# Copies in PSUM for the low parts of three more weights, and one sum of squares a tick sooner, in a hybrid decoder block on Trainium2

## The chip, the cores and the metric

The kernel runs on one core of a Trainium2 chip. The metric is the device time of one execution in microseconds (us), given as the median of several executions. A core has five engines that run side by side: TensorE (PE in the profile, with its weight loads as PEld) multiplies matrices, VectorE (DVE), ScalarE (ACT) and GpSimd (POOL) work element by element, and SyncE (SP) issues the transfers. SBUF is the working memory, and PSUM the small memory in eight banks into which TensorE writes its sums.

## The reference

One layer over 512 tokens of width 2048: an RMS norm and one input projection, three token mixers (dilated attention, a convolution module, windowed attention), an output projection and the residual, and then a second RMS norm and a SwiGLU feed-forward part of width 5632. The change lies where the second norm meets the feed-forward part:

```
x = x + mix @ w_out[l]
h2 = _rms_norm(x, norm2_g[l])
x = x + (jax.nn.silu(h2 @ w_gate[l]) * (h2 @ w_up[l])) @ w_down[l]
```

## The kernel before, in words

Activations lie transposed, 128 channels by 512 tokens to a tile. The program is written out in order by Python code, and every engine executes its own instructions in exactly that order. What one engine needs of another is waited for with semaphores.

**Split weights.** Every fp32 weight tile of 128x1024 is split before use into a high part (`wh`, the tile rounded to fp32r) and a low part (`wl`, what the rounding lost), and TensorE multiplies with both. `split_up_to` does this two weights ahead of TensorE's use (`SPLIT_AHEAD`), in one of two ways. In the first (lines 244 and 245) ScalarE casts the weight into `wh`, and VectorE subtracts: `wl` = weight - `wh`, both inputs in SBUF. In the second (lines 247 to 250) ScalarE casts the weight twice, once into a copy in PSUM (`near`, in the trace `wn`) and once into `wh` in SBUF, and VectorE subtracts the PSUM copy from the weight. `wh` and `wl` have three buffers each (`SPLIT_BUFS`). The copies live in the pool `high`, which has two buffers of 128x1024.

**The feed-forward part** multiplies with a seven-product scheme (Strassen's). Each of its blocks, `g1`, `u1`, `g2`, `u2` and so on, takes seven weights in the order `ORDER` = (5, 1, 7, 6, 2, 4, 3). Four of the seven are sums of quarter matrices: in order they are the first s, 11, 21, s again, 12, 22, s again, where s is one buffer into which GpSimd adds more quarters between uses (`add`, line 193; for the first block some are VectorE's). I call them weights 1 to 7 of a block. With each weight TensorE does eight matmuls of 512 columns with `wh` and eight of 256 columns with `wl`. Which of the two comes first alternates: for weights 1 to 7 of `g1`, high, high, high, low, high, low, high (weights 1 and 2 are done in two halves each).

**The seam.** `g1` is the first block. While TensorE begins it, the last tiles of `x2` (the residual stream) are still being turned into operands: `add_x2` and `operands` run from a list of steps that fall due at ticks (`Ticks.after(n, ...)` queues a step n ticks ahead, and steps of one tick run in the order in which they were queued). The squares of all `x2` tiles are added into `ssum2` (the trace shows it as `ssum`), the last of them by VectorE. After weight 3, `norm2a` has TensorE add `ssum2` over the channels into the PSUM tile `n2s` (line 307), VectorE scales it (`n2v`, line 378) and GpSimd takes the power -1/2 (`n2r`, line 379). After weight 4, `norm2b` has TensorE spread the result over 128 partitions into the same tile (line 313), and ScalarE copies it to `r2b` (lines 969 and 970). The tile `n2s` occupies one of the two buffers of `high` from `norm2a` to the copies of `norm2b`. A block's finished products are taken out of PSUM by VectorE in `done`, one weight later.

The list of weights begins with `units`, those of the two projections. So `len(units)` is the number of weight 1 of `g1`, and `len(units) + len(ORDER)` that of weight 1 of `u1`. `next_unit` first runs the sums due, then the splits, then the loads (`pump`).

Of the kernel before, what the change touches and what calls it, by code (L numbers as in the profile page):

```python
# [64 lines left out]
ORDER = (5, 1, 7, 6, 2, 4, 3)  # L65
# [57 lines left out]
def kernel(ctx: ExitStack, tc: tile.TileContext, xT, wi, wo, wgu, wd, cst_in, outT):  # L123
# [18 lines left out]
    ticks = Ticks()  # L142

    def slot(name, dt=F32, cols=T):
        return sp.tile([P, cols], dt, name=name, tag="s")
# [8 lines left out]
    units = [wi[0][:, :T], wi[0][:, T:]] + [wi[u] for u in range(1, 2 * N_IN)]  # L154
# [15 lines left out]
    def drop(key):  # L170
        for buf in [b for b, k in held.items() if k == key]:
            held.pop(buf)
        return raws.pop(key)
# [61 lines left out]
    def split_up_to(i):  # L235
        while at["split"] <= min(i, len(works) - 1):
            key, last, eng = works[at["split"]]
            t, n = drop(key) if last else raws[key]
            u = at["split"]
            hi = wp.tile([P, 1024], F32R, name=f"wh{u}", tag="hi", bufs=SPLIT_BUFS)  # L240
            lo = wp.tile([P, 1024], F32R, name=f"wl{u}", tag="lo", bufs=SPLIT_BUFS)
            if eng or u < len(units) + len(ORDER):
                eng = eng or nc.vector
                nc.scalar.copy(hi[:, :n], t[:, :n])  # L244
                eng.tensor_sub(lo[:, :n], t[:, :n], hi[:, :n].bitcast(F32))  # L245
            else:
                near = psum["high"].tile([P, 1024], F32R, name=f"wn{u}", tag="h")
                nc.scalar.copy(near[:, :n], t[:, :n])
                nc.scalar.copy(hi[:, :n], t[:, :n])
                nc.vector.tensor_sub(lo[:, :n], t[:, :n], near[:, :n].bitcast(F32))  # L250
            splits[u] = (hi, lo)
            at["split"] += 1
# [5 lines left out]
    def next_unit(ahead=SPLIT_AHEAD):  # L258
        sums_now()
        u = at["use"]  # L260
        at["use"] += 1
        split_up_to(u + ahead)
        pump(RAW_EARLY if u < 20 else RAW_BUFS)
        return splits.pop(u)
# [16 lines left out]
    for k in range(X_AHEAD):  # L281
        load_first(k)
        u = k if k < 2 else k // 2 + 1
# [100 lines left out]
    for k in range(2):  # L384
        h_hl[k] = scaled(xs[k], col(C_G1 + k), "h", k)
        split_up_to(k)
# [427 lines left out]
    ssum2 = slot("ssum2")  # L814
# [12 lines left out]
    def halves(t):  # L827
        return t[:, :TH], t[:, TH:]
# [22 lines left out]
    def scale_x2(n):  # L851
        t = x2.pop(n)
        h2[n], sq = slot(f"h2_{n}"), slot(f"sr{n}")
        nc.scalar.activation(h2[n], t, AF.Copy, scale=col(C_G2 + n))  # L854
        if n < KT - 1:
            nc.scalar.activation(sq if n else ssum2, t, AF.Square)
            ticks.after(1, add_x2, n, sq)
        else:
            nc.vector.tensor_add(ssum2, ssum2, h2.pop("square"))
            ticks.after(1, nc.scalar.activation, sq, t, AF.Square)  # L860
            add_x2(n, sq)

    def add_x2(n, sq):
        j = n % NJ
        eng = nc.gpsimd if n < KT - 2 else nc.vector
        if n < NJ:
            tops[j] = slot(f"ta{j}")
            (h11, h12), n1 = halves(h2[j]), tops[j][:, :TH]
            eng.tensor_sub(n1, h11, h12)  # L869
            ticks.after(1, operands, j, (1, h11), (5, n1))  # L870
        else:
            (h11, h12), (h21, h22) = halves(h2.pop(j)), halves(h2.pop(n))
            ta, tb = tops.pop(j), slot(f"tb{j}")
            n3, (n2, n4) = ta[:, TH:], halves(tb)
            eng.tensor_sub(n3, h12, h22)
            eng.tensor_sub(n2, n3, h11)
            eng.tensor_add(n4, n2, h21)
            if n < KT - 1:
                ticks.after(1, operands, j, (7, n3), (6, n2), (2, h21))
                ticks.after(2, operands, j, (4, n4), (3, h22))  # L880
            else:
                ticks.after(0, operands, j, (7, n3), (6, n2))
                ticks.after(2, eng.tensor_add, ssum2, ssum2, sq)
                ticks.after(2, operands, j, (2, h21), (4, n4), (3, h22))
        if n == NJ - 1:
            ticks.after(1, nc.vector.tensor_add, ssum2, ssum2, sq)
        elif n == KT - 2:
            h2["square"] = sq
        elif 0 < n < KT - 1:
            ticks.after(1, eng.tensor_add, ssum2, ssum2, sq)  # L890
# [425 lines left out]
```

## Time and profile before

| | |
|---|---|
| median of 3 executions | 1894.49 us (1893.85 to 1895.07) |
| the profiled execution | 1893.63 us, its span 1891.8 us |
| TensorE busy | 1883.8 us (100% of the span) |
| VectorE, ScalarE, GpSimd busy | 1450.7, 1317.2, 1174.1 us |
| `g1` begins on TensorE | 597.0 us after the span's start |
| DMA | 317.67 MB, mean 168 GB/s |

The median stands 0.86 us above the profiled execution, and the profiled execution 1.8 us above its span. A row of the timeline gives start, duration, engine, line, operation, out<-in; behind it, in brackets, how long the engine was idle before it and what ended that. Rows that follow each other at once are merged (x8), and the duration of a merged row of matmuls reaches to the modelled end of the last, which overlaps with the next row's start. For TensorE the distance from one row's start to the next is therefore the better measure of what a row takes.

### The profile page before, as it was taken

To read this page: it belongs to the slowest core of one execution; us is meant where nothing else is said; L and a number is where in the kernel's file an instruction comes from. 1 tells how busy PE (TensorE), PEld (TensorE's weight loads), DVE (VectorE), ACT (ScalarE), POOL (GpSimd) and SP (SyncE) were. 2 spreads that over 40 slices of the span, in tenths; PEclk is the share of its full clock that TensorE was granted. 3 is DMA by queue.
4 is the path that set the end of the run, shared out by engine and by line. 5 is a ranking of instruction groups with operands and counts; after the bars stand their busy time and mean duration, and the time that the engine had idled before them with its cause. 6 is when DMAs were issued, how large, how long until landed. Compare 5 with 4: busy or idle time off the path is not lost.

```text
span 1891.8 us, 29715 instructions
## 1 busy us (share of the span) xinstructions
PE 1883.8 (100%) x10342; PEld 1638.5 (87%) x10342; DVE 1450.7 (77%) x2419; ACT 1317.2 (70%) x1841; POOL 1174.1 (62%) x795
## 2 busy tenths in 40 slices
PE   9999999999999999999999999999999999999999
PEld 7888888888888888888888888888888888888888
DVE  7788888997579777777777777777777876767777
ACT  6355654453465788888888788888887866666776
POOL 5134423331055878787778788788787654656777
PEclk9999999999999999999999999999999999999999
DMA  7343333334342354443544445454547766767777
GB/s 269 87 124 98 84 99 102 102 95 145 113 144 88 114 172 146 160 164 131 180 136 165 158 151 167 134 180 138 167 151 275 269 227 233 273 231 270 275 260 242
DMA packets 134246, 317.67 MB, mean 168 GB/s; under 512 B 15312, under 2 KB 30800, under 8 KB 134096
## 3 DMA queue, kind: packets, MB, share of 16 engines
q1 hardware_dynamic: 133952, 315.68, 50.2%
q8 instruction: 81, 1.33, 0.3%
q14 instruction: 69, 0.57, 0.1%
q10 hardware_dynamic: 144, 0.10, 0.0%
HBM read 252.28 MB, written 55.84 MB: 163 GB/s over the span
## 4 chain that ended last, share of the span: by engine, by line
PE 98%; DVE 1%; issue 0%; ACT 0%; DVEq 0%
PE out L1006 67%; PE o L267 3%; PE o L268 3%; PE o L269 3%; PE cq L267 2%; PE cq L269 2%; PE cq L268 2%; PE aq L267 1%; PE aq L269 1%; PE ak L267 1%; PE ak L269 1%; PE in L267 1%; PE av L269 1%; PE av L268 1%; PE av L267 1%; PE aq L268 1%
## 5 line engine op out<-in xcount | busy, mean ns | idle before, releaser
L1006 PE MATMUL out<-h,wh 128*128 128x512 f32 x2464 | 588.4, 391 | 0.0
L1006 PEld LDWEIGHTS out<-h,wh 128*128 128x128 f32 x2464 | 452.7, 188 | 87.5
L1006 PEld LDWEIGHTS out<-h,wl 128*128 128x128 f32 x2464 | 316.1, 191 | 14.7 <-DVE wl L245 2.7
L1006 PE MATMUL out<-h,wl 128*128 128x256 f32 x2464 | 320.4, 283 | 2.1 <-DVE wl L245 2.1
L1006 PE MATMUL out<-a,wh 128*128 128x512 f32 x1232 | 295.9, 391 | 0.0
L1006 PEld LDWEIGHTS out<-a,wh 128*128 128x128 f32 x1232 | 225.8, 188 | 43.3
L244 ACT CAST wh<-w 128x1024 fp32r<-128x1024 f32 (+1 forms) x93 | 96.6, 1042 | 120.0 <-PE o L268 43.2
L1006 PEld LDWEIGHTS out<-a,wl 128*128 128x128 f32 x1232 | 159.4, 191 | 7.0
L1006 PE MATMUL out<-a,wl 128*128 128x256 f32 x1232 | 161.7, 283 | 0.0
L245 DVE TENSOR_TENSOR wl<-w,wh 128x1024 fp32r<-128x1024 f32 (+1 forms) x93 | 117.6, 1265 | 48.5 <-ACT wh L244 46.8
L450 DVE SCALAR_TENSOR_TENSOR y<-bu,cst,y 128x511 f32<-128x511 f32 (+14 forms) x120 | 90.1, 751 | 0.6
L1019 DVE TENSOR_TENSOR y<-y,out 128x256 f32<-128x256 f32 x93 | 39.1, 420 | 43.4 <-PE out L1006 36.9
L267 PE MATMUL cq<-hh,wh 128*128 128x512 f32 x128 | 51.2, 400 | 0.0
L267 PE MATMUL o<-mh_c,wh 128*128 128x512 f32 x128 | 50.8, 397 | 0.0
L269 PE MATMUL cq<-hh,wl 128*128 128x512 f32 x128 | 50.0, 391 | 0.0
L269 PE MATMUL o<-mh_c,wl 128*128 128x512 f32 x128 | 50.0, 390 | 0.0
L268 PE MATMUL cq<-hl,wh 128*128 128x512 f32 x128 | 49.9, 390 | 0.0
L268 PE MATMUL o<-ml_c,wh 128*128 128x512 f32 x128 | 49.9, 390 | 0.0
L1020 DVE TENSOR_TENSOR y<-y,out 128x256 f32<-128x256 f32 x101 | 42.5, 421 | 3.4
L371 POOL TENSOR_TENSOR ssum<-ssum,sq 128x512 f32<-128x512 f32 x15 | 27.3, 1818 | 18.7 <-ACT sq L370 18.1
L680 POOL TENSOR_SCALAR a3e<-a3e,a3d 128x128 f32<-128x128 f32 (+3 forms) x8 | 8.6, 1086 | 43.6 <-DVE a3d L678 39.0
L869 POOL TENSOR_TENSOR ta<-h 128x256 f32<-128x256 f32 x8 | 7.5, 933 | 43.6 <-ACT h L854 43.6
(3124 smaller groups left out, 4988.2 us busy)
## 6 DMA issues: line engine op xcount, KB each, us to landing
a<-od SPq DMA_DIRECT2D x168, 256.0 KB, 5.2
od<-a SPq DMA_DIRECT2D x147, 256.0 KB, 5.1
w<-in_wi SPq DMA_DIRECT2D x59, 512.0 KB, 3.7
w<-in_wo SPq DMA_DIRECT2D x32, 512.0 KB, 3.6
yd<-y SPq DMA_DIRECT2D x68, 128.0 KB, 2.7
y<-yd SPq DMA_DIRECT2D x34, 256.0 KB, 5.2
x<-in_xT SPq DMA_DIRECT2D x16, 256.0 KB, 7.5
xr<-in_xT SPq DMA_DIRECT2D x16, 256.0 KB, 3.9
```

Source lines behind the costliest of these rows:

```text
L244: nc.scalar.copy(hi[:, :n], t[:, :n])
L245: eng.tensor_sub(lo[:, :n], t[:, :n], hi[:, :n].bitcast(F32))
L267: nc.tensor.matmul(out, wh, xh, start=start, stop=False)
L268: nc.tensor.matmul(out, wh, xl, start=False, stop=False)
L269: nc.tensor.matmul(out, wl, xh, start=False, stop=stop)
L371: eng.tensor_add(acc, acc, sq)
L450: nc.vector.scalar_tensor_tensor(yconv[j][:, i:], hconv[j][:, :T - i], c, yconv[j][:, i:], op0=ALU.mult, op1=ALU.add)
L680: nc.gpsimd.tensor_scalar(e[:, o:o + n], e[:, o:o + n], rd[:, i:i + 1], None, op0=ALU.mult)
L869: eng.tensor_sub(n1, h11, h12)
L1006: nc.tensor.matmul(out, lhs[:, s], rhs, start=begin, stop=last and low == flip[0] and x is xs[-1], skip_group_check=True)
L1019: sign(out, out if first is None else first, main)
L1020: sign(out, out, rest)
```

## The change

Two edits. The first lowers the bound below which a weight of the feed-forward part is split in the first way: weights 5, 6 and 7 of `g1` are now split in the second way, with a copy in PSUM. Weights 1 to 4 of `g1` stay as they were, and from `u1` on nothing differs. The second has VectorE add the square of the last `x2` tile into `ssum2` one tick sooner.

```
@@ split_up_to, line 242
-            if eng or u < len(units) + len(ORDER):
+            if eng or u < len(units) + 4:
                 eng = eng or nc.vector
                 nc.scalar.copy(hi[:, :n], t[:, :n])
                 eng.tensor_sub(lo[:, :n], t[:, :n], hi[:, :n].bitcast(F32))
             else:
                 near = psum["high"].tile([P, 1024], F32R, name=f"wn{u}", tag="h")
...
@@ add_x2, line 883
                 ticks.after(0, operands, j, (7, n3), (6, n2))
-                ticks.after(2, eng.tensor_add, ssum2, ssum2, sq)
+                ticks.after(1, eng.tensor_add, ssum2, ssum2, sq)
                 ticks.after(2, operands, j, (2, h21), (4, n4), (3, h22))
```

On ScalarE, from the last operand cast (`h`) to the copies of the second norm, there stood before two casts, one each for weight 5 (`12`) and weight 6 (`22`) of `g1`; the rows end with weight 7 (`s`) and the first copy for `u1`:

```order
L833 CAST h_7_6019<-h_15_5916 128x256
L244 CAST wh_6065<-w('12', 'g1')_5658 128x1024
L244 CAST wh_6069<-w('22', 'g1')_5509 128x1024
L969 COPY r2b<-n2s 128x512
L970 COPY r2b<-n2s 128x256
L244 CAST wh_6101<-w('s', 'g1')_5709 128x1024
L248 CAST wn_6125<-w('s', 'u1')_6058 128x1024
```

The same place on ScalarE now, with the engines whose semaphores each instruction waits for (DVE_49 is VectorE's, PE_49 TensorE's, Pool_49 GpSimd's, DMAHW a transfer's):

```order
L833 CAST h_7_6019<-h_15_5916 128x256
L248 CAST wn_6067<-w('12', 'g1')_5658 128x1024 [waits DMAHW6_49]
L249 CAST wh_6065<-w('12', 'g1')_5658 128x1024 [waits PE_49]
L248 CAST wn_6073<-w('22', 'g1')_5509 128x1024 [waits DVE_49]
L249 CAST wh_6071<-w('22', 'g1')_5509 128x1024 [waits PE_49]
L969 COPY r2b<-n2s 128x512 [waits PE_49]
L970 COPY r2b<-n2s 128x256
L248 CAST wn_6107<-w('s', 'g1')_5709 128x1024 [waits DVE_49,Pool_49]
L249 CAST wh_6105<-w('s', 'g1')_5709 128x1024 [waits Activation_49]
L248 CAST wn_6131<-w('s', 'u1')_6058 128x1024 [waits Activation_49,Pool_49]
```

Three casts into PSUM (`wn`) are new. Since `n2s` holds one buffer of `high`, the copies of weights 5, 6 and 7 take turns in the other: the copy of weight 6 waits for VectorE (its subtraction for weight 5), and the copies into `r2b` stand behind it.

On VectorE, at the end of the operands, weight 4 of `g1` (`wl` of `s`) and the last addition into the sum of squares (`ssum`) change places:

```order
 L834 TENSOR_TENSOR h_7_5985<-ta_5851,h_7_5985 128x256
 L834 TENSOR_TENSOR h_7_5988<-tb_5920,h_7_5988 128x256
-L245 TENSOR_TENSOR wl_6001<-w('s', 'g1')_5709,wh_6000 128x1024
 L103 TENSOR_TENSOR ssum_4224<-ssum_4224,sr_5917 128x512
+L245 TENSOR_TENSOR wl_6002<-w('s', 'g1')_5709,wh_6001 128x1024
 L834 TENSOR_TENSOR h_7_6013<-h_15_5916,h_7_6013 128x256
 L834 TENSOR_TENSOR h_7_6016<-tb_5920,h_7_6016 128x256
```

The addition now stands ahead of the subtraction; nothing else moved there.

A little further on VectorE, the subtractions for weights 5, 6 and 7 read `wn` where they read `wh`, in the same places between the evacuations of `g1` (L1019, L1020):

```order
 L1019 TENSOR_TENSOR g1r<-g1r,out_5925 128x256
 L1020 TENSOR_TENSOR g1r<-g1r,out_5925 128x256
-L245 TENSOR_TENSOR wl_6066<-w('12', 'g1')_5658,wh_6065 128x1024
-L245 TENSOR_TENSOR wl_6070<-w('22', 'g1')_5509,wh_6069 128x1024
+L250 TENSOR_TENSOR wl_6066<-w('12', 'g1')_5658,wn_6067 128x1024
+L250 TENSOR_TENSOR wl_6072<-w('22', 'g1')_5509,wn_6073 128x1024
 L1019 TENSOR_TENSOR g1u<-g1u,out_5928 128x256
 L1020 TENSOR_TENSOR g1u<-g1u,out_5928 128x256
-L245 TENSOR_TENSOR wl_6102<-w('s', 'g1')_5709,wh_6101 128x1024
+L250 TENSOR_TENSOR wl_6106<-w('s', 'g1')_5709,wn_6107 128x1024
```

Only the second input and the line changed; TensorE, GpSimd and the transfers keep their order.

More of the change, by code (lines that the diff above doesn't have):

```diff
@@ L241, in split_up_to @@
             lo = wp.tile([P, 1024], F32R, name=f"wl{u}", tag="lo", bufs=SPLIT_BUFS)
-            if eng or u < len(units) + len(ORDER):
+            if eng or u < len(units) + 4:
                 eng = eng or nc.vector
@@ L882, in add_x2 @@
                 ticks.after(0, operands, j, (7, n3), (6, n2))
-                ticks.after(2, eng.tensor_add, ssum2, ssum2, sq)
+                ticks.after(1, eng.tensor_add, ssum2, ssum2, sq)
                 ticks.after(2, operands, j, (2, h21), (4, n4), (3, h22))
```

## The prediction

> **What bounds the kernel now.** I read the page first, for the engine that sets the end, then TensorE's waits, then the chain of waits, and then the timeline around the only place that these name. The page:
>
> ```profile
> span 1891.8 us, 29715 instructions
> PE 1883.8 (100%) x10342; PEld 1638.5 (87%) x10342; DVE 1450.7 (77%) x2419; ACT 1317.2 (70%) x1841; POOL 1174.1 (62%) x795
> PE 98%; DVE 1%; issue 0%; ACT 0%; DVEq 0%
> ```
>
> TensorE is busy all the time and makes up 98% of the chain that ended last. No edit here takes a matmul away, so the change can only give back time in which TensorE stands still. The view of waits, for TensorE alone, lists all such waits of the span (engine, line, what it waited for: total, times, longest):
>
> ```profile
> PE out L1006 <- DVE wl L245: 2.1, 1, 2.1
> PE idle L355 <- DVE warm L353: 1.8, 1, 1.8
> PE n2s L307 <- DVE ssum L103: 0.4, 1, 0.4
> ```
>
> The first and third lie at the edited lines; the second is the start of the program. The chain, in order of time, ends thus:
>
> ```profile
> 605.20 0.68 DVE ssum L103
> ...
> 608.99 6.44 DVE wl L245 x2
> 615.48 1272.62 PE out L1006 x7312
> ```
>
> After 615.48 us TensorE runs through 1272.62 us to the end without waiting. What it gains before that point it keeps, as long as the feeding engines come forward with it. The seam on TensorE, by the timeline:
>
> ```profile
> 604.43 1.11 PE L1006 MATMUL out<-h,wl 128*128 128x256 f32 x8
> 605.94 1.05 PE L307 MATMUL n2s<-ones,ssum 128*128 128x1 f32 x8 [0.40 <-DVE ssum L103]
> 606.86 1.21 PE L1006 MATMUL out<-h,wl 128*128 128x256 f32 x8
> ...
> 609.74 0.60 PE L313 MATMUL n2s<-ident,n2r 128*128 128x128 f32 x4
> 610.10 2.09 PE L1006 MATMUL out<-h,wh 128*128 128x512 f32 x8
> 612.17 1.21 PE L1006 MATMUL out<-h,wl 128*128 128x256 f32 x8
> 615.48 1.21 PE L1006 MATMUL out<-h,wl 128*128 128x256 f32 x8 [2.09 <-DVE wl L245]
> 616.53 3.82 PE L1006 MATMUL out<-h,wh 128*128 128x512 f32 x16
> 620.18 2.08 PE L1006 MATMUL out<-h,wl 128*128 128x256 f32 x16
> 622.09 3.82 PE L1006 MATMUL out<-h,wh 128*128 128x512 f32 x16
> ```
>
> From start to start, sixteen high matmuls take 620.18 - 616.53 = 3.65 us and sixteen low ones 622.09 - 620.18 = 1.91 us; eight take 1.825 and 0.955. By these, TensorE lost 605.94 - (604.43 + 0.955) = 0.55 us ahead of the sum of squares (0.40 by the profile's modelled end), 612.17 - (610.10 + 1.825) = 0.24 us ahead of weight 5's low matmuls, and 615.48 - (612.17 + 0.955) = 2.35 us ahead of weight 6's. The eight after that stall took 616.53 - 615.48 = 1.05 us, 0.10 more than eight in a row. All together this is 3.24 us, the most that the change can win.
>
> Why weight 6's low part came so late stands on VectorE (DVE) and GpSimd (POOL):
>
> ```profile
> 604.07 1.22 DVE L245 TENSOR_TENSOR wl<-w('s', 'g1')_5709,wh 128x1024 fp32r<-128x1024 f32 x1
> 605.20 0.68 DVE L103 TENSOR_TENSOR ssum<-ssum,sr 128x512 f32<-128x512 f32 x1
> 607.41 0.15 DVE L378 TENSOR_SCALAR n2v<-n2s 128x4 f32<-128x4 f32 x1
> 608.99 3.12 DVE L245 TENSOR_TENSOR wl<-w('12', 'g1')_5658,wh 128x1024 fp32r<-128x1024 f32 x1
> 612.04 3.38 DVE L245 TENSOR_TENSOR wl<-w('22', 'g1')_5509,wh 128x1024 fp32r<-128x1024 f32 x1
> ...
> 607.64 1.02 POOL L379 TENSOR_TENSOR n2r<-n2v,nhalf 128x4 f32<-128x4 f32 x1 [15.73 <-DVE n2v L378]
> 608.63 2.40 POOL L193 TENSOR_TENSOR w('s', 'g1')_5709<-w('s', 'g1')_5709,w('12', 'g1')_5658 128x1024 f32<-128x1024 f32 x1
> 610.98 3.36 POOL L193 TENSOR_TENSOR w('s', 'u1')_6058<-w('21', 'u1')_5971,w('22', 'u1')_5973 128x1024 f32<-128x1024 f32 x1
> 614.41 3.27 POOL L193 TENSOR_TENSOR w('21', 'u1')_5971<-w('21', 'u1')_5971,w('11', 'u1')_5975 128x1024 f32<-128x1024 f32 x1
> ```
>
> With GpSimd idle, the subtraction took 1.22 us (weight 4, at 604.07). Beside GpSimd's additions it took 3.12 and 3.38, and the rows interlock: weight 5's ends at 612.11, 1.08 us after the first addition (611.03), the second addition ends at 614.34, and weight 6's at 615.42, again 1.08 us later. The two take turns, 6.50 us for what alone would be 2.44.
>
> **The change part by part.** The copies in PSUM first. Their price stands further on, where weights already go that way and GpSimd is adding at the same time:
>
> ```profile
> 621.40 1.01 ACT L248 CAST wn<-w('11', 'u1')_5975 128x1024 fp32r<-128x1024 f32 x1
> 622.34 1.04 ACT L249 CAST wh<-w('11', 'u1')_5975 128x1024 fp32r<-128x1024 f32 x1
> 622.44 1.22 DVE L250 TENSOR_TENSOR wl<-w('11', 'u1')_5975,wn 128x1024 fp32r<-128x1024 f32 x1 [1.15 <-ACT wn L248]
> 622.82 2.42 POOL L193 TENSOR_TENSOR w('s', 'u1')_6058<-w('s', 'u1')_6058,w('11', 'u1')_5975 128x1024 f32<-128x1024 f32 x1
> ```
>
> Subtraction and addition overlap from 622.82 to 623.66 and neither is longer than alone (1.22 and 2.42). So the subtractions fall from 3.12 and 3.38 to 1.22. What the change adds is three casts of 1.01 us on ScalarE (ACT), and a new wait: the copy of weight 6 must wait until the subtraction of weight 5 has read its buffer, with the copies into `r2b` and weight 7's casts queued behind it. ScalarE there, before:
>
> ```profile
> 602.42 0.63 ACT L103 ACTIVATE sr<-xr 128x512 f32<-128x512 f32 x1
> ...
> 604.82 1.04 ACT L244 CAST wh<-w('12', 'g1')_5658 128x1024 fp32r<-128x1024 f32 x1
> 605.77 1.04 ACT L244 CAST wh<-w('22', 'g1')_5509 128x1024 fp32r<-128x1024 f32 x1
> 610.38 0.59 ACT L969 COPY r2b<-n2s 128x512 f32<-128x512 f32 x1 [3.57 <-PE n2s L313]
> 610.86 0.38 ACT L970 COPY r2b<-n2s 128x256 f32<-128x256 f32 x1
> 611.12 1.06 ACT L244 CAST wh<-w('s', 'g1')_5709 128x1024 fp32r<-128x1024 f32 x1
> 614.37 1.02 ACT L248 CAST wn<-w('s', 'u1')_6058 128x1024 fp32r<-128x1024 f32 x1 [2.19 <-POOL w('s', 'u1')_6058 L193]
> ```
>
> Worked through: weight 5's casts start at 604.82 as now and end by 606.8, inside ScalarE's 3.57 us of idle time. Its subtraction keeps its start, 608.99, since VectorE is busy up to there, and ends at 610.20. A hand-over between engines takes 0.03 us (cast end 622.41, subtraction 622.44). So weight 6's copy runs from 610.23 to 611.24, its subtraction from 611.27 to 612.49, and TensorE can start on it 0.05 us later (as it did after 615.42), at 612.54 instead of 615.48: **2.94 us sooner**.
>
> Does TensorE reach that point by then? This is the second edit. The addition into `ssum` moves ahead of weight 4's subtraction; it is one VectorE instruction without a transfer, and its input is there (`sr` ends at 603.05). It starts at 604.07 and ends at 604.75, before TensorE is free at 605.39, so TensorE's wait goes. Weight 4's subtraction then ends near 605.9; it is wanted after the eight `n2s` matmuls (606.86 - 605.94 = 0.92 us), at 605.39 + 0.92 = 606.31: 0.4 us of cover. `n2v` and `n2r` gain nothing, since VectorE's own queue brings `n2v` to 607.41. TensorE goes on, by the distances of the rows, to 609.19 for the spread (`n2r` ends at 608.66), 609.55 for weight 5's high matmuls, 611.38 for its low ones (there since 610.20), and is at weight 6 by 612.33; with the profile's 0.40 in place of 0.55, by 612.48. It then waits 0.06 to 0.21 us for 612.54. With the addition left in its place it would come at 612.88, and the gain would be 2.60. So the sum is 2.60 for the copies and 0.34 for the tick; the tick alone, with the late subtraction still in place, would be worth nothing.
>
> What is late next: weight 6's second cast ends near 612.2, the two `r2b` copies take until 612.9, weight 7's two casts until 614.9. Weight 7's high part is wanted at 612.54 + 0.955 + 1.825 = 615.32, 0.4 us later. `r2b` is first read by GpSimd after its three additions; these, no longer held up, are through near 608.63 + 3 x 2.42 = 615.9. GpSimd's sum for weight 1 of `u1` is ready at 613.5 instead of 614.34, so that its copy on ScalarE is ready near 615.8 and its subtraction by 617.0, against a need at 615.32 + 1.825 + 0.955 = 618.1. From there all engines are about 2.9 us earlier than before, and their distances to each other stay.
>
> One rule speaks against the copies. The Trainium skill's page Perfetto Trace Analysis, section Optimizing Scalar/DVE Operations, puts the overhead of a VectorE instruction at about 60 ns for SBUF and about 125 ns for PSUM, and that of ScalarE at about 93 and 51 ns. By it the two subtractions would cost 0.13 us more and the copy between them 0.04 less, and the gain would be 2.85 us, an estimate from that page. The rows here show no difference: 1.22 us from SBUF alone (604.07) and 1.22 us from PSUM (622.44), and the sum goes by the rows.
>
> The profiled execution's 1893.63 us so becomes 1890.7. Its span would be near 1888.9. The median stood 0.86 us above it, so that I expect a median of 1894.49 - 2.94, rounded to 1891.6.
>
> **The rivals.** 0.2% of the time, about what a measurement of this kernel can tell from no change, is 3.79 us; even the 3.24 us of all stalls stays within it.
>
> *A part is given back* (1892.0 to 1894.0, I take 1893.0): the new serial stretch of ScalarE (copy, cast, two `r2b` copies, copy, cast) has only 0.4 us of cover at weight 7, and weight 4's subtraction 0.4. If a hand-over there costs 1 us more than the rows say, TensorE waits there instead. For it: nothing in the trace shows this stretch yet. Against it: every piece has a row, and the hand-overs measure 0.03 to 0.05.
>
> *The subtraction from PSUM still takes turns with GpSimd*, as its other input is still in SBUF. Then weight 5's ends at 612.11 as now, weight 6's copy at 613.15, and its subtraction, behind the second addition (614.5), at 615.6: 0.2 us later than now, 1894.7. Against it stand the rows at 622.44 and 622.82.
>
> *Slower:* they take turns, and GpSimd's next addition goes ahead of the waiting subtraction each time. Weight 5's then ends after two additions, at 613.45 + 1.1 = 614.6, and its copy for weight 6 at 615.6; two more additions' worth (the third ends at 615.9, the next 2.4 later) puts weight 6's subtraction at 619.4, and TensorE at 619.5, 4.0 us later than now: 1898.5. It decides against the change from the point where weight 5's subtraction ends later than 613.1, 2.9 us after what I expect. The additions would have to follow each other at once, and the rows at 608.99 to 615 show the two engines in strict turn.
>
> *More than all stalls:* the gain passes 3.79 us, 1890.5. It would need stalls that these records don't show, in other executions perhaps (the median is 0.86 us above this one), or elsewhere in the 1272.62 us that the chain shows without a wait.
>
> **How the numbers follow.** Forecast 0.78; a part given back 0.06; still in turn 0.03; slower 0.06; more than all stalls 0.07. The forecast's own range is 2.4 to 3.24 us of gain and the 0.6 us by which single runs stray, 1890.8 to 1892.5; to hold 8 in 10 with the edges of its neighbours I give 1890.6 to 1893.4. Faster by over 0.2% is the last case, 0.07; slower 0.06; within 0.2% the other three, 0.87.
>
> **What would show it.** Right: the subtractions of weights 5 to 7 at line 250 with 1.22 us each, the additions of line 193 at 2.4 us, no TensorE wait on `ssum`, and weight 6's low matmuls starting near 612.5 with a wait below 0.3 us. Wrong: a subtraction at line 250 over 2 us, a wait of TensorE for `wh` at weight 7, for ScalarE at `u1`, or a new wait later than 616 us.

## The result, and the profile after

Measured side by side in 14 executions each, the changed kernel takes 1890.43 us (1889.87 to 1891.26) and the kernel before 1894.29 us (1893.19 to 1895.45). The ratio is 0.9981 with a 95% interval of 0.9972 to 0.9989: 3.86 us faster, with the interval reaching from 2.1 to 5.3 us. In a second comparison (the changed kernel 11 times, the kernel before 33 times) the medians are 1891.13 and 1893.93 us, 2.80 us apart, ratio 0.9986 (0.9977 to 0.9995). All executions of the study taken together (25 and 107) give medians of 1890.82 and 1893.99 us, 3.17 us apart. The forecast was a gain of 2.94 us, a median of 1891.6 us in a range of 1890.6 to 1893.4: the first median lies 0.17 us below that range, the second inside it.

The page of the changed kernel and TensorE's waits in it:

```profile
span 1888.5 us, 29717 instructions
PE 1882.8 (100%) x10342; PEld 1638.2 (87%) x10342; DVE 1444.8 (77%) x2419; ACT 1319.8 (70%) x1844; POOL 1170.3 (62%) x795
```

```profile
PE idle L355 <- DVE warm L353: 1.8, 1, 1.8
```

Of the three waits of TensorE only the program's start is left in this view. The span is 3.3 us shorter. The seam on TensorE, by the timeline (the last row is a weight load, PEld):

```profile
596.74 1.07 PE L1006 MATMUL out<-h,wh 128*128 128x512 f32 x4
...
604.14 1.12 PE L1006 MATMUL out<-h,wl 128*128 128x256 f32 x8
605.10 0.95 PE L307 MATMUL n2s<-ones,ssum 128*128 128x1 f32 x8
605.91 1.20 PE L1006 MATMUL out<-h,wl 128*128 128x256 f32 x8
...
611.07 2.43 PE L1006 MATMUL out<-h,wl 128*128 128x256 f32 x16
613.33 3.82 PE L1006 MATMUL out<-h,wh 128*128 128x512 f32 x16
...
612.28 1.01 PEld L1006 LDWEIGHTS out<-h,wl 128*128 128x128 f32 x8 [0.30 <-DVE wl L250]
```

In this execution `g1` begins at 596.74 us, before it began at 597.03. Over all profiles of this study that start lies between 596.29 and 597.59 us, though nothing ahead of it was changed: single executions stray by that much before the seam. So I count from the start of `g1`. Weight 6's low part is begun 15.54 us after it (612.28, by its weight load, since the row of its matmuls is merged with weight 5's), where its matmuls began after 18.45 us (615.48, 0.01 us behind their weight load). The following high matmuls stand at 613.33 - 596.74 = 16.59 us against 19.50: **2.91 us of the gain are there**. VectorE, GpSimd and ScalarE at the seam:

```profile
603.78 0.69 DVE L103 TENSOR_TENSOR ssum<-ssum,sr 128x512 f32<-128x512 f32 x1
...
608.70 1.21 DVE L250 TENSOR_TENSOR wl<-w('12', 'g1')_5658,wn 128x1024 fp32r<-128x1024 f32 x1
611.00 1.22 DVE L250 TENSOR_TENSOR wl<-w('22', 'g1')_5509,wn 128x1024 fp32r<-128x1024 f32 x1 [1.08 <-ACT wn L248]
...
608.35 2.40 POOL L193 TENSOR_TENSOR w('s', 'g1')_5709<-w('s', 'g1')_5709,w('12', 'g1')_5658 128x1024 f32<-128x1024 f32 x1
610.70 2.42 POOL L193 TENSOR_TENSOR w('s', 'u1')_6058<-w('21', 'u1')_5971,w('22', 'u1')_5973 128x1024 f32<-128x1024 f32 x1
613.20 2.41 POOL L193 TENSOR_TENSOR w('21', 'u1')_5971<-w('21', 'u1')_5971,w('11', 'u1')_5975 128x1024 f32<-128x1024 f32 x1
...
609.95 1.02 ACT L248 CAST wn<-w('22', 'g1')_5509 128x1024 fp32r<-128x1024 f32 x1 [3.43 <-DVE wl L250]
613.54 1.07 ACT L249 CAST wh<-w('s', 'g1')_5709 128x1024 fp32r<-128x1024 f32 x1
```

The subtractions take 1.21 and 1.22 us in place of 3.12 and 3.38, the additions 2.40 to 2.42 in place of up to 3.36, and each engine passes the other without a hold. The new wait is where it was expected: ScalarE stands 3.43 us until the subtraction for weight 5 has read its buffer, time in which it stood idle before too.

### The profile page after: what moved, and what is told of

Its sections match the earlier page's. It is cut to its first block, busy times and chain, and to the rows that moved or that the text cites. A ratio compares the mean times of both kernels' runs of the same rounds, so it can differ in the third digit from the quotient of the medians.

```text
span 1888.5 us, 29717 instructions
## 1 busy us (share of the span) xinstructions
PE 1882.8 (100%) x10342; PEld 1638.2 (87%) x10342; DVE 1444.8 (77%) x2419; ACT 1319.8 (70%) x1844; POOL 1170.3 (62%) x795
## 4 chain that ended last, share of the span: by engine, by line
PE 98%; DVE 1%; issue 0%; ACT 0%; DVEq 0%
PE out L1006 67%; PE o L268 3%; PE o L267 3%; PE o L269 3%; PE cq L267 2%; PE cq L269 2%; PE cq L268 2%; PE aq L267 1%; PE aq L269 1%; PE ak L267 1%; PE ak L269 1%; PE av L267 1%; PE av L269 1%; PE av L268 1%; PE ak L268 1%; PE aq L268 1%
## 5 line engine op out<-in xcount | busy, mean ns | idle before, releaser
L1019 DVE TENSOR_TENSOR y<-y,out 128x256 f32<-128x256 f32 x93 | 39.0, 420 | 43.4 <-PE out L1006 37.1
L1020 DVE TENSOR_TENSOR y<-y,out 128x256 f32<-128x256 f32 x101 | 42.5, 421 | 3.5
```

The lines of the kernel that those rows point to most:

```text
L1019: sign(out, out if first is None else first, main)
L1020: sign(out, out, rest)
```

## The experiments

Where an experiment's file has more lines than the kernel's, its line numbers are higher by up to eight.

**The copies alone.** The second edit is undone: `ticks.after(2, eng.tensor_add, ssum2, ssum2, sq)`.

> The three copies in PSUM, with the addition into the sum of squares left where it was before. My theory: the subtractions of weights 5 to 7 take 1.22 us, TensorE still waits 0.4 us (0.55 by row starts) for the sum of squares, comes to weight 6's low matmuls later than these are ready, and so waits nowhere else at the seam. Gain over the kernel before 2.6 us, 1891.7 us. Rival, that the tick carries the gain or that the two need each other: 1893.5 to 1894.3 us. Rival, that there is a gain beyond the seam: below 1891 us.

Measured: 1891.26 us (11 executions), ratio 0.9985 (0.9976 to 0.9994). TensorE's waits, and its rows at the seam:

```profile
PE n2s L307 <- DVE ssum L103: 0.4, 1, 0.4
```

```profile
597.01 1.07 PE L1006 MATMUL out<-h,wh 128*128 128x512 f32 x4
...
612.00 2.08 PE L1006 MATMUL out<-h,wl 128*128 128x256 f32 x16
613.91 3.82 PE L1006 MATMUL out<-h,wh 128*128 128x512 f32 x16
```

Weights 5 and 6 follow without a gap, and the next high matmuls stand 613.91 - 597.01 = 16.90 us after the start of `g1` against 19.50 before: 2.60 us, as the sum had it. The time agrees (2.84 us below the kernel before). So the copies alone carry most of the gain: the tick adds 2.91 - 2.60 = 0.31 us by the rows, which is too little for the times to show.

**The tick alone.** The first edit is undone: `if eng or u < len(units) + len(ORDER):`.

> The addition into the sum of squares one tick sooner, with weights 5 to 7 of g1 split in SBUF as before. My theory: TensorE no longer waits for the sum of squares (0.4 us), and waits as much longer for weight 6's low part, which is late for another reason: it starts at the same distance from the start of g1 as before (18.45 us), and the time is that of the kernel before, 1894.3 us. Rival, that the sooner sum lets GpSimd's chain start sooner: up to 0.5 us faster, with GpSimd's power of the norm starting before 607.3 us.

Measured: 1895.09 us, ratio 1.0007 (0.9998 to 1.0016), with 1894.1 us for the kernel before: 1.0 us more, with no change still inside the interval. TensorE, by the timeline, and the view of windows, where the number behind the five engines' busy times is the granted TensorE clock:

```profile
596.46 1.07 PE L1006 MATMUL out<-h,wh 128*128 128x512 f32 x4
...
611.60 1.21 PE L1006 MATMUL out<-h,wl 128*128 128x256 f32 x8 [0.65 <-DVE wl L245]
614.91 1.22 PE L1006 MATMUL out<-h,wl 128*128 128x256 f32 x8 [2.10 <-DVE wl L245]
615.96 5.43 PE L1006 MATMUL out<-h,wh 128*128 128x512 f32 x16
621.23 2.07 PE L1006 MATMUL out<-h,wl 128*128 128x256 f32 x16
```

```profile
613.00:615.00 2.00, 0.09 (x1) 0.09 (x1) 2.00 (x2) 1.19 (x2) 1.92 (x2) 1.00 0.62 217
615.00:617.00 2.00, 2.00 (x12) 1.76 (x13) 1.97 (x3) 0.80 (x1) 2.00 (x1) 0.82 0.00 0
617.00:619.00 2.00, 2.00 (x6) 1.61 (x5) 2.00 (x3) 0.00 (x0) 1.82 (x3) 0.50 0.00 0
619.00:621.00 2.00, 2.00 (x8) 1.55 (x8) 1.68 (x3) 0.72 (x2) 1.26 (x2) 0.83 0.00 0
621.00:623.00 2.00, 2.00 (x17) 1.95 (x16) 1.14 (x2) 2.00 (x3) 2.00 (x2) 1.00 0.00 0
```

The first part came as expected: the wait on `ssum` is gone, and weight 6 begins 614.91 - 596.46 = 18.45 us after the start of `g1`, to the hundredth as before. But then sixteen high matmuls take 621.23 - 615.96 = 5.27 us in place of 3.65. The granted clock is 0.50 for a while: 0.82, 0.50 and 0.83 over three windows of 2 us are about 0.7 + 2.0 + 0.7 = 3.4 us at half speed, which costs 1.7 us. Nothing like it stands in the profiles of the kernel before and after. The executions' mean clocks tell how often it happens: it rounds to 0.999 or 0.998 in 10 of 11 executions of this kernel, to 0.999 in 19 of the 93 of the kernel before for which it was recorded (7 of the 33 beside this kernel), and to 1.000 in all 25 of the changed kernel. So the change in the clock is clear where that of the median is not. The rounding hides a stretch that costs less than some 0.9 us (0.0005 of the span).

**The same casts, with the high part read from SBUF.** The changed kernel, where the subtraction of weights 5 to 7 doesn't use the copy:

```
-                nc.vector.tensor_sub(lo[:, :n], t[:, :n], near[:, :n].bitcast(F32))
+                second = hi if u < len(units) + len(ORDER) else near
+                nc.vector.tensor_sub(lo[:, :n], t[:, :n], second[:, :n].bitcast(F32))
```

> Both edits, but the subtractions of weights 5 to 7 read the high part in SBUF in place of the copy in PSUM; the three copies are still made and not read, so ScalarE's work and order are those of the changed kernel, without its wait for VectorE. My theory, that the place of the second input is what counts: the subtractions of weights 5 and 6 take 3.1 and 3.4 us again and take turns with GpSimd's additions, and TensorE stands 2.1 to 2.6 us before weight 6's low matmuls; 1894.3 us. Rival, that the casts' new order or the spacing of the subtractions makes the gain: 1.2 us each and about 1891 us.

Measured: 1896.68 us (1893.37 to 1897.48), ratio 1.0008 (0.9999 to 1.0017). Its VectorE rows:

```profile
609.38 3.12 DVE L251 TENSOR_TENSOR wl<-w('12', 'g1')_5658,wh 128x1024 fp32r<-128x1024 f32 x1
612.43 3.39 DVE L251 TENSOR_TENSOR wl<-w('22', 'g1')_5509,wh 128x1024 fp32r<-128x1024 f32 x1
```

The long subtractions are back with nothing in the program but the place of the second input changed, and with them TensorE's gaps of 0.65 and 2.10 us. (ScalarE's copy of weight 6 no longer waits for VectorE and comes sooner, at 607.11.) So the place of that input decides; the next experiment asks for the other half, GpSimd's part. In 8 of 11 executions the clock fell here too. The three in which it rounds to 1.000 have a median of 1893.45 us, the two at 0.999 1894.87, and the six at 0.998 1896.99: steps of 1.4 and 3.5 us, as of one and of two stretches of 3.4 us at half speed.

**GpSimd's additions taken away.** In the kernel before, `add` returns for `g1`'s quarter 12 and for quarter 21 of `u1`, and makes the first sum of `u1` by `nc.gpsimd.memset(out[:, :n], 0.0)`.

> The kernel before, with GpSimd's three additions at the seam taken away: the one into g1's sum and the one that finishes quarter 21 of u1 are left out, and the one that makes u1's sum is a memset, so the results of g1 and u1 are not the reference's. My theory: without an addition beside them the subtractions of weights 5 and 6 take 1.22 us from SBUF too, TensorE does not wait for weight 6, and keeps the 0.4 us wait for the sum of squares: 2.6 us faster than before, 1891.7 us, without any copy in PSUM. If a memset, which only writes, holds VectorE up as well, weight 5's subtraction is up to 2.4 us longer and part of the stall stays. Rival, that the subtractions are slow for another reason (what TensorE or ScalarE read at that time): 3.1 and 3.4 us as before, 1894.3 us.

Measured: 1891.45 us, ratio 0.9984 (0.9975 to 0.9993). VectorE and GpSimd:

```profile
609.23 1.22 DVE L252 TENSOR_TENSOR wl<-w('12', 'g1')_5658,wh 128x1024 fp32r<-128x1024 f32 x1
610.37 1.22 DVE L252 TENSOR_TENSOR wl<-w('22', 'g1')_5509,wh 128x1024 fp32r<-128x1024 f32 x1
...
608.86 0.96 POOL L196 MEMSET w('s', 'u1')_6057<- 128x1024 f32 x1
```

Without the additions the subtractions take 1.22 us from SBUF too, and the gain is that of the copies, without a copy. So it was the additions that held them, and only while both inputs lay in SBUF. The memset, which only writes, lies beside the first subtraction from 609.23 to 609.82 and holds nothing up.

**TensorE's gaps filled with useless work.** The tick alone once more, with matmuls ahead of weights 5 and 6 whose result goes to a part of the `n2s` tile that is no longer read:

```
+                if self.name == opening and low and q in FILL:
+                    for _ in range(FILL[q]):
+                        nc.tensor.matmul(spare[0], ops[5, 0][:, :P], ops[5, 0], start=True, stop=True)
...
+    FILL = {2: 2, 4: 9}
```

> The tick alone, as in tick_only, and eleven more matmuls of 128x512 on TensorE whose result nobody reads: two ahead of weight 5's low matmuls (0.46 us in a gap of 0.74) and nine ahead of weight 6's (2.05 us in a gap of 2.35). Theory: in tick_only TensorE's granted clock fell to 0.5 for some 4 us after the two gaps, because TensorE had been idle for most of 5 us; with the gaps filled by useless work the clock stays at 1.00 from 613 to 623 us and the median falls from 1895.1 to 1893.6 us, though TensorE does more. Rival, that the drop comes by chance or has its cause elsewhere: 1895.1 us again, with a clock below 1.00 after the seam in most executions. Rival, that the matmuls themselves delay weight 6: more than 1895 us with the clock at 1.00.

Measured: 1893.54 us (1892.76 to 1893.92), where the tick alone had 1895.09 (1893.10 to 1896.86), and a mean clock of 1.000 in 11 of 11 executions. The two were measured in different comparisons, on different chips; against the kernel before, in its own comparison, this kernel stands 0.39 us lower (ratio 0.9998, 0.9989 to 1.0006) and the tick alone 0.99 us higher. The kernel before fell about as often on both chips (7 of 33 and 12 of 60). TensorE and its clock:

```profile
612.99 2.23 PE L1009 MATMUL n2s<-h 128*128 128x512 f32 x9
615.26 1.21 PE L1014 MATMUL out<-h,wl 128*128 128x256 f32 x8
616.31 3.81 PE L1014 MATMUL out<-h,wh 128*128 128x512 f32 x16
619.96 2.08 PE L1014 MATMUL out<-h,wl 128*128 128x256 f32 x16
```

```profile
617.00:619.00 2.00, 2.00 (x10) 1.67 (x9) 2.00 (x2) 0.00 (x0) 2.00 (x2) 1.00 0.00 0
```

Weight 6 comes no sooner (18.45 us after the start of `g1`, at 596.81), but the sixteen matmuls after it take 3.65 us again. More work on TensorE kept its clock up and made the kernel about 1.4 us faster, taken against the kernel before in each comparison.

**Only one of the two gaps filled.** `FILL = {2: 2, 4: 0}` and `FILL = {2: 0, 4: 9}`.

> The tick alone with only the smaller gap filled: two idle matmuls ahead of weight 5's low ones, TensorE still standing 2.1 to 2.35 us before weight 6. Theory: it takes both gaps within 5 us for the clock to fall often, so this behaves like the kernel before, which has one large gap there and a small one: a clock below 1.00 in few executions (about 1 in 6), 1893.9 us. Rival, that the large gap alone does it: a clock below 1.00 in most executions, 1895 us, as with the tick alone.

> The tick alone with only the larger gap filled by nine idle matmuls, the gap of 0.65 to 0.74 us ahead of weight 5's low matmuls left. Theory: with the large gap filled the clock never falls: 1893.5 us, all executions at 1.000, as with both filled.

Measured with the small gap filled: 1893.60 us, the clock below 1.000 in 3 of 11. With the large gap filled: 1894.10 us (1892.98 to 1895.74), the clock at 1.000 in 11 of 11. On the clock both came as expected: the large gap alone lets it fall now and then, both together nearly always, the small one alone in none of 11. The second's time did not: 0.6 us above what I expected, with no drop. That is within the interval of the comparison (ratio 1.0001, 0.9992 to 1.0010). Its profile shows one wait of 0.3 us on a later weight, 1785.70 us into the span. The experiment with one cast more, below, shows what that wait is and that its length differs between executions; whether it makes up the 0.6 us stays open.

**The kernel before with its gaps filled.** The same eleven matmuls, the tick not moved.

> The kernel before, the tick not moved, with the same eleven idle matmuls ahead of weights 5 and 6. Theory: the part of the gain that goes beyond the removed stalls comes from executions of the kernel before in which the clock fell after the large gap; with the gap filled none falls, the median is 1893.5 us instead of 1894.0, and the highest execution stays below 1894.7. (The two idle matmuls ahead of weight 5 meet a gap of only 0.24 us and can delay it by 0.2 us; weight 6 is late anyway.) Rival, that the clock plays no part in the kernel before: 1894.0 us with the same spread as before.

Measured: 1893.42 us (1892.80 to 1894.06), ratio 0.9995 (0.9986 to 1.0004), the clock at 1.000 in 11 of 11; beside it the kernel before had 1894.06 us (1892.86 to 1895.78), with 8 of 27 at 0.999. The long tail of the kernel before is gone. None of 11 against 8 of 27 could by itself still be chance; with the two other kernels whose large gap was filled it is none of 33 against 19 of 93. The shift of the median, 0.6 us, is within the interval of no change, so that this part of the gain is shown in the clock and the spread, and its size only roughly.

**The evacuation behind the subtractions.** In the changed kernel, for weight 4 of `g1`, `run(evacs)` goes behind `next_unit`.

> The changed kernel, with VectorE's evacuation of weight 3's products after the subtractions of weights 5 and 6 in place of ahead of them (1.5 us of work that nothing waits for there). Theory: weight 5's subtraction starts at 607.2 in place of 608.7 us, its copy for weight 6 follows, weight 6's low part is ready before TensorE is, and the last 0.25 us of waiting at the seam goes: 0.25 us faster than the changed kernel, 1890.2 us, and no TensorE wait at line 1006 for weights or evacuation. Rival: the late evacuation holds weight 6's matmuls, which add onto the bank that it reads: a TensorE wait for VectorE's reduction, no gain.

Measured: 1890.44 us, ratio to the kernel before 0.9981 (0.9972 to 0.9990); the changed kernel beside it 1891.13 us, 0.9986 (0.9977 to 0.9995). The two intervals overlap, so the times don't tell them apart. The profile does, at the seam:

```profile
596.37 1.07 PE L1006 MATMUL out<-h,wh 128*128 128x512 f32 x4
...
610.70 2.08 PE L1006 MATMUL out<-h,wl 128*128 128x256 f32 x16
612.61 3.82 PE L1006 MATMUL out<-h,wh 128*128 128x512 f32 x16
```

Weights 5 and 6 now follow without a gap, and the next matmuls stand 16.24 us after the start of `g1` in place of 16.59: 0.35 us sooner. This is the last of the seam's waiting. The profiled execution doesn't keep it: from those matmuls to the end it takes 1889.2 - 612.61 = 1276.59 us, the changed kernel 1888.5 - 613.33 = 1275.17, because TensorE loses time again further on (0.41 us of it in a wait for a weight's low part, at 1769.69 us). So this version is better at the seam, and not shown to be better as a whole.

**One cast more on ScalarE.** In the changed kernel weight 6's second cast is done twice.

> The changed kernel with weight 6's second cast on ScalarE done twice (1.0 us more in the serial stretch of ScalarE). My theory of the cover: weight 7's high part is then ready 0.4 to 0.5 us after TensorE needs it, a new wait on ScalarE at weight 7, 0.3 to 0.5 us slower than the changed kernel (1890.9 us). If the stretch had more room than I think: no wait and the same time as the changed kernel. If it had none, 1.0 us slower.

Measured: 1891.49 us, beside 1891.13 for the changed kernel, a difference within the intervals. The new wait stands where it was forecast:

```profile
612.88 2.00 PE L1008 MATMUL out<-h,wh 128*128 128x512 f32 x8
615.29 2.12 PE L1008 MATMUL out<-h,wh 128*128 128x512 f32 x8 [0.40 <-ACT wh L249]
617.24 2.08 PE L1008 MATMUL out<-h,wl 128*128 128x256 f32 x16
```

By row starts the gap is 615.29 - (612.88 + 1.825) = 0.58 us, so 0.47 us of the added 1.05 us were covered. In the changed kernel's rows the cast for weight 7 ended at 614.61 and was wanted at 613.33 + 1.825 = 615.16, 0.55 us later.

This profile has a second wait of TensorE, longer than the first, 1168 us later. The chain that ended last runs through it:

```profile
1769.22 6.70 DMA w('22', 'd18')_18480<-in_wd
1775.98 2.14 POOL w('s', 'd18')_18542 L193
...
1782.54 1.09 DVE wl L252
1783.68 102.67 PE out L1008 x588
```

`d18` is one of the last blocks. GpSimd waits for the transfer of its quarter 22, makes its first sum from it at 1775.98 us (in the changed kernel's profile at 1773.67), VectorE's work behind that comes later, and TensorE stands still for 0.99 us. By row starts the fourteen low matmuls of this place take 1784.62 - 1781.70 = 2.92 us, where they take 1.68 in the changed kernel (1783.01 - 1781.33). In the kernel before they took 1.83, and in five of the other experiments 1.9 to 2.2. So the place costs from nothing to 1.2 us, although no experiment changes anything there. It is a second cause, beside the clock, for executions of one kernel to differ; how often it acts and whether the change makes it more frequent is not shown.

**The changed kernel once more.**

> The changed kernel once more, beside the others: 1890.4 us, granted clock 1.000 in every execution.

Measured: 1891.13 us (1890.43 to 1892.21), the clock at 1.000 in 11 of 11. The time is 0.7 us above that of the first 14 executions; `g1` began at 597.59 us in its profile, 0.85 us later than in the first.

## Why the prediction was right

- *The number.* The forecast gain of 2.94 us stands beside 3.86 and 2.80 measured. The 3.86 passes even the 3.79 us from which the prediction counted its last rival, "more than all stalls", but its interval, 2.1 to 5.3 us, holds both that and the forecast. So the times neither confirm 2.94 nor rule that rival out, and since the changed kernel's own two medians lie 0.70 us apart, it is partly luck how near any of them comes. What bears the prediction out is the rows at the seam.
- *What bounds the kernel.* Right in the two profiles: from the high matmuls behind the seam to the end the kernel before takes 1891.8 - 616.53 = 1275.27 us and the changed kernel 1275.17, so the gain at the seam (2.91 us) is there at the end. The condition that the prediction set, that the feeding engines come forward too, isn't met in every execution of the variants: near 1783 us a late transfer held TensorE for up to 0.99 us, in the profile with the added cast.
- *Why weight 6's low part was late.* Right, and shown both ways: it is long wherever its second input lies in SBUF and GpSimd adds (3.12 and 3.39 us), and 1.22 us when either the input is in PSUM or the additions are gone.
- *The sum.* Weight 6 was forecast 15.51 us after the start of `g1` (612.54 - 597.03), measured 15.54; the copies' part 2.60, measured 2.60 at the next high matmuls (at weight 6's own start, 612.00 + 0.955 - 597.01 = 15.945 us, it is 2.50; eight low matmuls that need not wait then take 0.10 us less). The subtraction, the copy and the subtraction ahead of weight 6 each began within 0.02 us of the forecast, counted from `g1`. The wait left ahead of weight 6 was put at 0.21 us by row starts; it is 612.28 - (611.07 + 0.955) = 0.25. Two terms on the way were off by the same amount and cancel, which is luck: the `n2s` matmuls took 0.81 us in place of 0.92, and weight 5's high ones 1.93 in place of 1.825.
- *Each edit's worth.* The step that failed is "the tick alone, with the late subtraction still in place, would be worth nothing". Its first half holds: weight 6 is no sooner. But the time not spent waiting for `ssum` is added to the gap ahead of weight 5, and the two gaps so close together bring the clock down in 10 of 11 executions, at a price of about 1.7 us by the windows. The medians, 1895.09 us against 1894.1, point the same way without being clear of noise. The prediction read one execution, in which the clock didn't fall, and had no term for it.
- *The ceiling.* "The most that the change can win" was put at 3.24 us, from the stalls of one execution. With the evacuation behind the subtractions, where no wait is left, the seam gives 19.50 - 16.24 = 3.26 us, so the total was right. Of its 0.24 us ahead of weight 5 some 0.11 were no wait: the row before takes 612.00 - 610.06 = 1.94 us in the copies alone too, where nothing waits. The `n2s` matmuls' 0.11 us, left out of the sum, make up for it. The stalls have a second price that this execution didn't show, the slower clock after them, in about a fifth of the executions of the kernel before. On average that is some 0.2 us (19 of 93 executions, 1.1 us above the others by their medians), which with the 2.91 us makes 3.1, between the 2.80 and the 3.86 us of the two comparisons. The rival "more than all stalls" had looked to executions other than the profiled one and to the long stretch behind the seam. Both were places worth looking: the clock is found in the one and the late transfer in the other. What is measured of the clock doesn't bring the sum to 3.79 us; what the late transfer adds or takes on average is not known.
- *What is late next.* Right: weight 7's high part, with 0.55 us of cover by the rows where 0.4 were forecast, and an added cast of 1.05 us makes that wait, 0.58 us long.

## What to carry to other kernels

When two engines run the same kind of operation on SBUF side by side and both grow long, see whether their ends interlock; if they do, try one input of the critical one in PSUM, which removed the hold here; it needs a third engine with the time to make the copy. A wait removed ahead of a later wait needn't be neutral: it moves idle time to where it may add up with another gap, so take away the later one first. Read the granted clock of all executions, not of the profiled one alone, before calling a gap's price its length. And look through the whole chain of each run: a difference of a few tenths between two variants can come from a transfer a thousand microseconds behind the edit.

## What was not expected of the hardware

TensorE's clock fell to half for 3.4 us where 0.65 and 2.10 us of waiting lay within some 4 us, with matmuls between (18 of 22 executions of two kernels). With one gap of 2.1 us and at most some 0.35 us by row starts just ahead of it, it fell in about one execution in five (22 of 104, the kernel before and the tick alone with its small gap filled). With matmuls in the large gap it fell in none of 33, and with the large gap removed in none of 69. The Trainium skill's page TensorE: Matmul & The Clock Gate, section Part 1: The HAM clock gate, says that the clock goes to half after an idle window of about 3.4 us and comes back after a busy one. The length of the slow stretch agrees (3.4 us in the tick alone; 0.52, 0.50, 0.50 and 0.77 over 8 us, or 6.8 us, twice that, in the kernel that reads the high part, below). The condition differs: no gap here reached 3.4 us, and the advice of no idle gaps over about 3 us, in its section Why this matters for your kernels, would have passed both. Why some executions have two slow stretches and others none, at the same gaps, was not settled. The drop isn't tied to the end of a gap: by the windows shown, the clock fell at about 617 - 0.72 = 616.3 us in the tick alone, 1.4 us after its large gap ended (614.91), and at about 617 - 1.92 = 615.1 us in the kernel that reads the high part, 0.8 us before its large gap ended (615.88). In the second, TensorE was still idle when the slow stretch began, and the stretch was twice as long; two profiles don't show that the one follows from the other.

```profile
615.00:617.00 2.00, 1.12 (x5) 1.13 (x6) 1.97 (x4) 1.76 (x2) 2.00 (x1) 0.52 0.22 90
617.00:619.00 2.00, 2.00 (x8) 1.74 (x8) 2.00 (x1) 0.00 (x0) 2.00 (x2) 0.50 0.00 0
619.00:621.00 2.00, 2.00 (x6) 1.58 (x5) 1.87 (x3) 0.00 (x0) 1.82 (x2) 0.50 0.00 0
621.00:623.00 2.00, 2.00 (x8) 1.57 (x8) 1.05 (x3) 1.78 (x3) 1.26 (x2) 0.77 0.00 0
```
